# Out-projection of a hybrid trunk: seven products of 2x2 blocks with weight sums formed in memory, and a regrouped GLA output

## The chip, the cores and the metric

One core of a Trainium2 chip. The metric is the device time of one launch in microseconds. The core has TensorE (matrix products, PE in the profile; its weight loads are PEld), VectorE (DVE), ScalarE (ACT), GpSimd (POOL) and SyncE (SP, which here only starts transfers). Products gather in eight PSUM banks of 128 x 512 f32.

## What is computed

One layer of a trunk with three kinds of heads, on 512 tokens with 16 learned tokens ahead of them (528 in all), model width 2048, float32:

```python
h = rms_norm(x, norm_w)
proj = h @ w_in                            # 2048 x 7585
# columns of proj go to
#   6 gated DeltaNet heads   (q, k, v of 128; conv, silu; chunked delta rule)
#   5 GLA heads              (q, k of 64, v of 128; chunks of 64)
#   5 forgetting-attention heads ("fox"; q, k, v of 128; softmax with decay)
o_dn  = gated_head_norm(o_dn,  dz, dn_norm_w)     # normed o * w * silu(dz)
o_gla = gated_head_norm(o_gla, gz, gla_norm_w)
o_fox = o_fox * silu(fz)
o = concat([o_dn, o_gla, o_fox])[tokens]          # 512 x 2048, 16 heads of 128
y = x + o @ w_out                                 # 2048 x 2048
out = rms_norm(y, final_norm_w)                   # the 512 tokens
```

All large products are made in three: every operand is split into a float32r part (hi) and the rest (lo), and hi·hi, lo·hi and hi·lo are summed. One logical product of 128 x 128 by 128 x 512 is therefore three TensorE instructions.

## The kernel before, in words

**In-projection.** The 7585 columns go in 59 blocks of 128 columns (`inproj`, products on L168), in the order in which heads need them. Each block takes two weight tiles of 128 x 1024 (512 KB): `load_half` starts the transfer on SP's queue, and `split` makes the hi part by a ScalarE copy (L144) and the lo part by a VectorE subtraction (L145). raw, hi and lo have two buffers each. The result is transposed: rows are columns of the projection, columns are tokens.

**Heads.** DeltaNet heads go in two groups of three, then GLA heads in pairs (`gla_pair`), then the fox heads one by one (`fox_head`). Each head's gate block (`gate_z`) makes silu(z) into a 128 x 512 tile `zs`; GpSimd takes the first step of a silu (a maximum, L287), ScalarE three, VectorE the multiply. At a head's end its output is multiplied into that tile. In `gla_pair` the output `pgo` of each head is made of four 128-token blocks; for each block stands a product of 128 rows (L769, attention within the block) and behind it one of 64 rows (L770, the state).

**Order.** A scheduler places every engine's instructions by estimated times, splits ahead of other work. So in-projection products fill TensorE while heads wait on other engines, and under the last fox heads the out-projection's first quarter does.

**Out-projection.** w_out is taken in four quarters of 512 columns (`cc`), and in each over 16 heads and four blocks of 128 tokens: `mms` (L913) issues the three products. Two heads share a weight tile of 512 KB (`rawo`, `whio`, `wloo` are its raw, hi and lo), so a tile feeds 24 products. `split_o` splits each head's output once. The last two heads (`LAST = 14`) are held back: their products (`pz`) come at the end, token block by token block, so that the adds to the residual (L972), the squares (L974), the norm (L978 to L984) and the output transfers (L990) of one token block run under the products of the next. The residual x is loaded on ScalarE's queue into `acc`. In the last token block the last quarter is cut in two halves of 256.

Of the kernel before, what the change touches and what calls it, by code (L numbers as in the profile page):

```python
# [8 lines left out]
F32 = mybir.dt.float32  # L9
F32R = mybir.dt.float32r  # L10
# [8 lines left out]
P = 128  # L19
# [8 lines left out]
H = 3  # L28
# [4 lines left out]
DN_HEADS, GLA_HEADS, FOX_HEADS = 6, 5, 5  # L33
R0 = 32
# [43 lines left out]
def tile_hybrid_trunk(ctx, tc, xT, xtok, mtok, w_gate, w_in, w_out, consts, lmask, fin_w, out, dbg=None):  # L78
# [5 lines left out]
    hp = pool("hp", 2 * KT)  # L84
    wp = pool("wp", 2)
    zp = pool("zp", 11)
    six = pool("six", 8)
    wk = pool("wk", 2)
# [4 lines left out]
    def row(name, dt=F32):  # L93
        return wk.tile([P, 3 + T], dt, tag="row", bufs=7, name=name)
# [83 lines left out]

    done = {}
# [113 lines left out]
    zs = {}  # L293

    def gate_z(kind, h, t=None):
# [4 lines left out]
        if t is None:  # L300
            t = zp.tile([P, S], F32, tag="zs", name=f"zs{kind}{h}")
        silu(t, z[:, :S], f"{kind}{h}")
        zs[kind, h] = t
# [335 lines left out]
    def gla_pair(p):  # L639
# [125 lines left out]
        for e in range(ne):  # L765
            rr = slice(64 * e, 64 * e + 64)
            for b in range(NB):
                bs = slice(b * P, (b + 1) * P)
                PE.matmul(po[e][:, bs], at[:, e * NB + b, :], vt[:, e, bs], start=True, stop=False)  # L769
                PE.matmul(po[e][:, bs], qd[rr, bs], ss[b][rr, :], start=False, stop=True)  # L770
        for e in range(ne):
            f = wk.tile([P, NB], F32, tag="gso", name=f"gso{p}{e}")
            for b in range(NB):
                sq = wk.tile([P, P], BF16, tag="sq", name=f"gsq{p}{b}{e}")
                A.activation(sq, po[e][:, b * P : (b + 1) * P], AF.Square, accum_out=f[:, b : b + 1])
            A.activation(f, f, AF.Ln, scale=1.0 / P, bias=eps_c)
            A.activation(f, f, AF.Exp, scale=-0.5)
            on = qk[:, e, :S]
            for b in range(NB):
                A.activation(on[:, b * P : (b + 1) * P], po[e][:, b * P : (b + 1) * P], AF.Copy, scale=f[:, b : b + 1])  # L780
            pt = psm.tile([P, 512], F32, tag="m", name=f"pgt{p}{e}")
            for b in range(NB):
                PE.transpose(pt[:, b * P : (b + 1) * P], on[:, b * P : (b + 1) * P], ident)
            o = zs["gz", 2 * p + e]
            V.scalar_tensor_tensor(out=o, in0=pt, scalar=glw[:, 0:1], in1=o, op0=ALU.mult, op1=ALU.mult)


    def fox_head(h):
# [22 lines left out]
        cc = six.tile([P, 2 * T + S], F32, tag="six", name=f"fc{h}")  # L811
        z = wk.tile([P, S], F32, tag="gd", name=f"fz{h}") if h < 2 else cc[:, T + S : T + 2 * S]
        gate_z("fz", h, z)
# [53 lines left out]
        V.tensor_tensor(out=z, in0=po[:, :512], in1=z, op=ALU.mult)  # L867
# [10 lines left out]
    for h in range(GLA_HEADS):  # L878
        gate_z("gz", h)
# [8 lines left out]
    for p in range(3):  # L888
        gla_pair(p)
    for h in range(GLA_HEADS):  # L890
        dump(f"ogl{h}", zs["gz", h])
    for h in range(FOX_HEADS):
        fox_head(h)
    for h in range(FOX_HEADS):
        dump(f"ofx{h}", zs["fz", h])


    heads = [("dz", h) for h in range(DN_HEADS)] + [("gz", h) for h in range(GLA_HEADS)] \
        + [("fz", h) for h in range(FOX_HEADS)]
    oparts = []  # L900

    def split_o(i):
        z = zs[heads[i]]
        hi, lo = part(f"oh{i}"), part(f"ol{i}")
        A.copy(hi, z)
        V.tensor_tensor(out=lo, in0=z, in1=hi.bitcast(F32), op=ALU.subtract)
        oparts.append((hi, lo))

    def mms(p_, hi, lo, i, tb, first, last):
        s = slice(tb * P, (tb + 1) * P)  # L910
        oh, ol = oparts[i]
        for n, (o_, w_) in enumerate(((oh, hi), (oh, lo), (ol, hi))):
            PE.matmul(p_, o_[:, s], w_, start=(first and n == 0), stop=(last and n == 2))  # L913

    LAST = 14
    halves = lambda w: [[t[:, j * 512 : (j + 1) * 512] for t in w] for j in range(2)]
    acc, wl = {}, {}

    def load_last(c):
        raw = wp.tile([P, 1024], F32, tag="raw", name=f"rawl{c}")  # L920
        nc.sync.dma_start(out=raw, in_=w_out[c, LAST // 2])
        r = []
        for j in range(2):
            hi, lo = part(f"wlh{c}{j}"), part(f"wll{c}{j}")
            split(raw[:, j * 512 : (j + 1) * 512], hi, lo)
            r.append((hi, lo))
        return r

    for i in range(LAST):
        split_o(i)  # L930
    for cc in range(4):
        pa = [psb.tile([P, 512], F32, tag="b", name=f"pa{cc}{tb}") for tb in range(4)]
        for kp in range(LAST // 2):
            w = halves(load_half(w_out[cc, kp], f"o{cc}_{kp}"))
            for j in range(2):
                i = 2 * kp + j
                for tb in range(4):
                    mms(pa[tb], *w[j], i, tb, i == 0, cc < 3 and i == LAST - 1)
            if cc == 3 and kp % 2 and kp < 6:
                c = kp // 2  # L940
                wl[c] = load_last(c)
        for tb in range(4):
            if 4 * cc + tb < 11:
                a = zp.tile([P, S], F32, tag="zs", name=f"acc{cc}{tb}")
            else:
                a = six.tile([P, S], F32, tag="six", name=f"acc{cc}{tb}")
            nc.scalar.dma_start(out=a, in_=xtok[tb * P : (tb + 1) * P, cc * 512 : (cc + 1) * 512])
            if cc < 3:
                V.tensor_tensor(out=a, in0=a, in1=pa[tb], op=ALU.add)
            acc[tb, cc] = a  # L950
        if cc == 0:
            for i in range(LAST, KT):
                split_o(i)
    wl[3] = halves(load_half(w_out[3, LAST // 2], "l3"))
    fw = []
    for c in range(4):
        f = part(f"fw{c}").bitcast(F32)
        nc.scalar.dma_start(out=f, in_=fin_w[c * 512 : (c + 1) * 512].partition_broadcast(P))
        fw.append(f)
    ss = wk.tile([P, 4, 5], F32, tag="fss", bufs=1, name="fss")  # L960
    rr = wk.tile([P, 4], F32, tag="frs", bufs=1, name="frs")
    for tb in range(4):
        for cc in (3, 0, 1, 2):
            a = acc[tb, cc]
            cuts = 2 if (tb, cc) == (3, 2) else 1
            for n in range(cuts):
                c = slice(512 // cuts * n, 512 // cuts * (n + 1))
                p_ = pa[tb] if cc == 3 else psm.tile([P, 512], F32, tag="m", name=f"pz{tb}{cc}{n}")
                for j in range(2):
                    hi, lo = wl[cc][j]  # L970
                    mms(p_[:, c], hi[:, c], lo[:, c], LAST + j, tb, cc < 3 and j == 0, j == 1)
                V.tensor_tensor(out=a[:, c], in0=a[:, c], in1=p_[:, c], op=ALU.add)  # L972
                sq = row(f"sqf{tb}{cc}{n}")
                A.activation(sq[:, c], a[:, c], AF.Square, accum_out=ss[:, tb, cc + 2 * n : cc + 2 * n + 1])  # L974
            if cc != 2:
                G.tensor_tensor(out=a, in0=a, in1=fw[cc], op=ALU.mult)  # L976
        r = rr[:, tb : tb + 1]
        V.reduce_sum(r, ss[:, tb, : 3 + cuts], axis=mybir.AxisListType.X)  # L978
        A.activation(r, r, AF.Ln, scale=1.0 / D, bias=eps_c)
        A.activation(r, r, AF.Exp, scale=-0.5)  # L980
        for cc in (3, 0, 1, 2):
            a = acc[tb, cc]
            if cc == 0:
                A.activation(a, a, AF.Copy, scale=r)  # L984
            elif cc == 2:
                V.scalar_tensor_tensor(out=a, in0=a, scalar=r, in1=fw[cc], op0=ALU.mult, op1=ALU.mult)  # L986
            else:
                V.tensor_scalar_mul(a, a, r)  # L988
            q = nc.scalar if cc % 2 else nc.sync
            q.dma_start(out=out[tb * P : (tb + 1) * P, cc * 512 : (cc + 1) * 512], in_=a)  # L990
# [55 lines left out]
```

## Time and profile before

| | us |
|---|---|
| median of 3 runs | 1047.62 (1046.19 to 1048.34) |
| the profiled execution | 1048.64 |
| its span, first to last instruction | 1046.9 |
| TensorE busy | 1019.8, granted clock 0.991 |
| VectorE busy | 574.8 |
| ScalarE busy | 410.7 |
| GpSimd busy | 134.9 |

How to read it. The page's row of slices gives the busy share of each of 40 equal parts of the span in tenths, PEclk the clock that TensorE was granted. A group line gives: line, engine, operation, output<-inputs with shapes, count, then busy time in all and the mean of one in ns, then the engine's idle time just before them and what ended most of it. A line of the list of waits gives what waited for what, then us in total, times, and the longest. A line of the chain or the timeline starts with start and duration in us. A table of stretches gives each engine's busy time with its count of instructions, the granted clock, the DMA share and GB/s.

### The profile page before, as it was taken

The numbers are of one execution on the slowest core, as the hardware profiler recorded it, in microseconds if no ns is written. First come the engines' busy times: TensorE is split into PE (matmuls) and PEld (weight loads), VectorE is DVE, ScalarE is ACT, GpSimd is POOL, SyncE is SP. The second block draws the span as 40 slices with busy tenths as digits, with TensorE's granted clock in tenths as the row PEclk, the third lists the DMA queues.
The fourth block names the chain that finished last, engine by engine and source line by source line (L and its number), as shares of the span: only waits on it lengthen the run. The fifth ranks groups of instructions, "written<-read, shape, count | busy, mean of one in ns | idle before, by whom it ended". The sixth has DMA issues, their size and how long they took to land.

```text
span 1046.9 us, 19027 instructions
## 1 busy us (share of the span) xinstructions
PE 1019.8 (97%) x7787; PEld 914.5 (87%) x7787; DVE 574.8 (55%) x1251; ACT 410.7 (39%) x895; POOL 134.9 (13%) x137
## 2 busy tenths in 40 slices
PE   9999999999999999999999999999999999999994
PEld 7899999989999888899989878898989888888883
DVE  6366868855567972334828274455444474332437
ACT  6643533343455333244344443333323262222234
POOL 0021312220213131000100010110101010000014
PEclk9999999999999998999999999999999999999998
DMA  9613222223222322222212122222222263222424
GB/s 351 233 48 127 82 89 92 99 77 108 89 69 82 96 102 77 69 77 73 78 42 67 46 87 74 94 72 86 89 84 87 86 204 126 93 82 100 141 81 160
DMA packets 42347, 105.15 MB, mean 100 GB/s; under 512 B 10589, under 2 KB 13917, under 8 KB 42260
## 3 DMA queue, kind: packets, MB, share of 16 engines
q1 hardware_dynamic: 26848, 90.23, 24.6%
q10 hardware_dynamic: 15412, 13.70, 4.5%
q8 instruction: 61, 1.00, 0.4%
q14 instruction: 26, 0.21, 0.1%
HBM read 98.74 MB, written 5.05 MB: 99 GB/s over the span
## 4 chain that ended last, share of the span: by engine, by line
PE 54%; DVE 3%; ACT 1%; issue 1%; DMA 0%; DVEq 0%
PE pp L168 29%; PE pa L913 15%; PE pss L708 1%; PE pgo L770 1%; PE pfo L863 1%; PE pgo L769 1%; PE pfa L831 1%; PE pz L913 1%; DVE acc L988 1%; PE pfx L846 1%; ACT sqf L974 0%; PE pfd L832 0%; PE pfo L866 0%; DVE acc L986 0%; PE pgk L660 0%
## 5 line engine op out<-in xcount | busy, mean ns | idle before, releaser
L168 PE MATMUL pp<-xh,whi 128*128 128x264 f32 (+2 forms) x1456 | 378.5, 312 | 0.9 <-DVE vg L278 0.8
L168 PE MATMUL pp<-xh,wlo 128*128 128x264 f32 (+2 forms) x1456 | 376.8, 311 | 0.0
L168 PE MATMUL pp<-xl,whi 128*128 128x264 f32 (+2 forms) x1456 | 376.2, 310 | 0.0
L168 PEld LDWEIGHTS pp<-xh,whi 128*128 128x128 f32 x1456 | 244.5, 190 | 16.0 <-issue 1.4
L168 PEld LDWEIGHTS pp<-xl,whi 128*128 128x128 f32 x1456 | 245.2, 190 | 14.4 <-issue 1.4
L168 PEld LDWEIGHTS pp<-xh,wlo 128*128 128x128 f32 x1456 | 245.4, 190 | 13.3 <-issue 0.3
L145 DVE TENSOR_TENSOR wlo<-raw,whi 128x1024 fp32r<-128x1024 f32 x110 | 136.4, 1240 | 124.6 <-ACT whi L144 123.8
L144 ACT CAST whi<-raw 128x1024 fp32r<-128x1024 f32 x110 | 115.3, 1049 | 202.2 <-PE pp L168 181.1
L913 PE MATMUL pa<-whio,ol 128*128 128x512 f32 x224 | 88.0, 393 | 0.0
L913 PE MATMUL pa<-wloo,oh 128*128 128x512 f32 x224 | 87.9, 393 | 0.0
L913 PE MATMUL pa<-whio,oh 128*128 128x512 f32 x224 | 79.1, 396 | 0.0
L145 DVE TENSOR_TENSOR wloo<-rawo,whio 128x1024 fp32r<-128x1024 f32 x28 | 34.6, 1236 | 75.2 <-ACT whio L144 75.1
L144 ACT CAST whio<-rawo 128x1024 fp32r<-128x1024 f32 x28 | 29.4, 1049 | 93.7 <-PE pa L913 60.1
L913 PEld LDWEIGHTS pa<-whio,ol 128*128 128x128 f32 x224 | 42.1, 188 | 9.9
L913 PEld LDWEIGHTS pa<-wloo,oh 128*128 128x128 f32 x224 | 42.1, 188 | 9.5
L913 PEld LDWEIGHTS pa<-whio,oh 128*128 128x128 f32 x224 | 42.0, 188 | 9.2
L287 POOL TENSOR_SCALAR stc<-cv 128x528 f32<-128x528 f32 (+1 forms) x18 | 28.3, 1572 | 165.3 <-DVE cv L361 142.5
L361 DVE SCALAR_TENSOR_TENSOR cv<-pb,cpk,cv 128x528 f32<-128x528 f32 (+1 forms) x54 | 40.8, 755 | 0.6
L976 POOL TENSOR_TENSOR acc<-acc,fw 128x512 f32<-128x512 f32 x12 | 15.7, 1335 | 170.9 <-ACT sqf L974 170.9
L278 DVE TENSOR_TENSOR pb<-pp,rstd 128x264 f32<-128x264 f32 (+1 forms) x36 | 13.8, 424 | 26.2 <-PE pp L168 26.1
L456 DVE TENSOR_TENSOR ot<-ab 51x30 f32<-51x30 f32 (+14 forms) x60 | 20.3, 339 | 3.3 <-POOL stc L287 1.7
L458 DVE TENSOR_TENSOR ab<-ab,ot 51x30 f32<-51x30 f32 (+14 forms) x60 | 20.6, 343 | 1.5
(380 smaller groups left out, 1304.2 us busy)
## 6 DMA issues: line engine op xcount, KB each, us to landing
raw<-in_w_in SPq DMA_DIRECT2D x110, 512.0 KB, 3.2
rawo<-in_w_out SPq DMA_DIRECT2D x28, 512.0 KB, 3.2
xt<-in_xtok SPq DMA_DIRECT2D x8, 512.0 KB, 9.1
acc<-in_xtok ACTq DMA_DIRECT2D x16, 256.0 KB, 5.4
xs<-in_xT SPq DMA_DIRECT2D x7, 528.0 KB, 6.8
rawl<-in_w_out SPq DMA_DIRECT2D x4, 512.0 KB, 5.2
out<-acc SPq DMA_DIRECT2D x8, 256.0 KB, 2.5
out<-acc ACTq DMA_DIRECT2D x8, 256.0 KB, 2.6
```

The costliest lines, as they stand in the source:

```text
L144: A.copy(hi, raw)
L145: V.tensor_tensor(out=lo, in0=raw, in1=hi.bitcast(F32), op=ALU.subtract)
L168: PE.matmul(p_[:, :nt], wt[:, j * m : (j + 1) * m], xx[k][:, t0 : t0 + nt], start=(k == 0 and wt is hi and xx is xh), stop=(k == KT - 1 an ...
L278: V.tensor_tensor(out=o, in0=p_[rows], in1=rstd[rows, t0 : t0 + n], op=ALU.mult)
L287: G.tensor_scalar_max(t, src, LOW)
L361: V.scalar_tensor_tensor(out=c, in0=pb[:, t0 + w : w + T], scalar=cwc[:, blk, w : w + 1], in1=c, op0=ALU.mult, op1=ALU.add)
L456: V.tensor_tensor(out=t3, in0=a3[:, j + 1 :, j : j + 1].to_broadcast([NN * 4 + H, m, j]), in1=a3[:, j : j + 1, 0:j].to_broadcast([NN * 4 + ...
L458: V.tensor_tensor(out=a3[:, j + 1 :, 0:j], in0=a3[:, j + 1 :, 0:j], in1=t3, op=ALU.add)
L708: PE.matmul(ps[o0 : o0 + n, b * n : b * n + n], kx[rr, k0 : k0 + n], qx[rr, q0 : q0 + n], start=True, stop=True)
L769: PE.matmul(po[e][:, bs], at[:, e * NB + b, :], vt[:, e, bs], start=True, stop=False)
L913: PE.matmul(p_, o_[:, s], w_, start=(first and n == 0), stop=(last and n == 2))
L976: G.tensor_tensor(out=a, in0=a, in1=fw[cc], op=ALU.mult)
```

## The change

**Out-projection.** Tokens are cut in two halves of 256, heads in two halves of eight, and two column quarters (`ca`, `cb`) make a pair. For each of the two pairs the 2x2 product of blocks is made by seven products of blocks instead of eight (a form of Strassen's scheme): a and f use plain blocks on both sides (a with its sign changed), b, c and e sums on both sides, d a sum of weights, g a sum of operands. Each product sums eight heads for two token blocks of 128 (`product`, `mms`). In PSUM, y gathers a and c, later e and g; z gathers b and d; intermediate values are added to or subtracted from several `acc` tiles (`add`).

**Weight sums.** Four sums of weight quarters for each pair, 2 MB each, are formed in device memory: a copy from w_out or from an earlier sum on SP's queue, then an accumulating transfer on GpSimd's queue, each in two parts of 1 MB and in pieces of 512 bytes. One of these steps is issued with each in-projection block from the 15th on; sum4's are eight blocks later than the rest. `load_w` loads tiles of 512 KB of a quarter or a sum; 56 are loaded, and each feeds 12 products. raw and hi have three buffers, lo two.

**Operands.** The sums of head outputs are made on VectorE (`sub`) and split by `put` (a ScalarE copy and a VectorE subtraction of 256 columns): n11, n1, t2, x22, n3, x21, n4, each of eight heads. The first nine heads' outputs are written to device memory (`spill`) and loaded again, two or three times, on GpSimd's queue (`load_o`), as is the residual.

**Gate blocks.** The gates of GLA heads 3 and 4 and of all fox heads are projected after the last fox head's other blocks; these heads' outputs are copied (`og`, `of`) and multiplied by silu(z) later.

**GLA grouping.** The products of `pgo` come in another order: those of 128 rows of both heads first, then those of 64 rows, the two heads (rows 0 to 63 and 64 to 127) in turn.

**The end.** The pair's product g is made token block by token block from kept weights (`last_w`), the last token block in halves of 256.

The order in which the program's instructions stand on each engine: by in-projection blocks counted from 0, one accumulation stands at block 26, four in a row at block 32 ahead of the `eg` multiplies (the decay times queries) of the second DeltaNet group, three at block 37 ahead of GLA's second `gkd`, four at block 44 around fox head 0's small copies, and the four of sum4 at blocks 50, 54, 54 and 58 between the last gates' maxima and the reloads. On ScalarE the copies of x22 stand ahead of the first weight tile's copy.

```diff
+    wsum = {(pr, n): drp.tile([4, P, 1024], F32, name=f"sum{n}_{pr}") for pr in range(2) for n in (1, 2, 3, 4)}
+    quarter = lambda pr, n: w_out[2 * pr + n // 2, 4 * (n % 2) : 4 * (n % 2) + 4]
...
+                def copy(pr=pr, h_=h_):
+                    tc.keep_in_program_order(nc.sync.dma_start(
+                        out=rows_of(wsum[pr, n][h_]), in_=rows_of(first(pr)[h_]), max_dma_last_dim=512))
...
+                def plus(pr=pr, h_=h_):
+                    tc.keep_in_program_order(nc.gpsimd.dma_start(
+                        out=rows_of(wsum[pr, n][h_]), in_=rows_of(then(pr)[h_]), accum_op=ALU.add,
+                        max_dma_last_dim=512))
...
+    one, three = list(sum_steps(1, q_(2), q_(3))), list(sum_steps(3, q_(0), q_(2)))
+    two, four = list(sum_steps(2, lambda pr: wsum[pr, 1], q_(0))), list(sum_steps(4, lambda pr: wsum[pr, 2], q_(1)))
+    steps = one[:4] + three[:4] + one[4:] + three[4:] + two + 8 * [lambda: None] + four
...
         if key not in done:
+            begun_blocks.append(key)
+            if len(begun_blocks) > 14 and steps:
+                steps.pop(0)()
...
         for e in range(ne):
-            rr = slice(64 * e, 64 * e + 64)
             for b in range(NB):
                 bs = slice(b * P, (b + 1) * P)
-                PE.matmul(po[e][:, bs], at[:, e * NB + b, :], vt[:, e, bs], start=True, stop=False)
-                PE.matmul(po[e][:, bs], qd[rr, bs], ss[b][rr, :], start=False, stop=True)
+                PE.matmul(po[e][:, bs], at[:, e * NB + b, :], vt[:, e, bs], start=b == 0, stop=False,
+                          skip_group_check=True)
+        for b in range(NB):
+            bs = slice(b * P, (b + 1) * P)
+            for e in range(ne):
+                rr = slice(64 * e, 64 * e + 64)
+                PE.matmul(po[e][:, bs], qd[rr, bs], ss[b][rr, :], start=False, stop=b == NB - 1,
+                          skip_group_check=True)
...
-        V.tensor_tensor(out=z, in0=po[:, :512], in1=z, op=ALU.mult)
+        o = zs["fz", h] = zp.tile([P, S], F32, tag="zs", name=f"of{h}")
+        A.copy(o, po[:, :512])
...
+    def put(op, i, src, sign=1.0):
+        hi, lo = (t[:, i] for t in op)
+        if sign > 0:
+            A.copy(hi, src)
+            V.tensor_tensor(out=lo, in0=src, in1=hi.bitcast(F32), op=ALU.subtract)
...
+    for h in range(GLA_NOW, GLA_HEADS):
+        gate_z("gz", h, zs["gz", h])
+    for h in range(FOX_HEADS):
+        gate_z("fz", h, zs["fz", h])
+    for i in range(KP):
+        a, b = load_o(i, "oa")
+        put(n11, i, a, -1.0)
+        put(n1, i, sub(f"d1_{i}", a, b))
+    for i in range(KP):
+        a, b = load_o(i, "ob")
+        c, d = load_o(KP + i, "oc")
+        u = sub(f"d2_{i}", a, b)
+        V.tensor_tensor(out=u, in0=u, in1=d, op=ALU.add)
+        put(t2, i, u)
...
+        put(x22, i, d)
+        put(n3, i, sub(f"d3_{i}", b, d))
+        put(x21, i, c)
...
+        product("a", y, n11, quarter(pr, 0), True, False)
...
+        product("b", z, n1, wsum[pr, 1], True, False)
...
+        product("c", y, t2, wsum[pr, 2], False, False)
...
+        product("d", z, x22, wsum[pr, 4], False, True)
...
+        product("e", y, n3, wsum[pr, 3], False, False)
...
+        product("f", w_, x21, quarter(pr, 1), True, True)
...
+        if pr == 0:
+            product("g", y, n4, quarter(pr, 3), False, True)
...
+                    for i in range(KP):
+                        mms(y[tb], n4, last_w[i], i, tb, False, n == cuts - 1 and i == KP - 1, cs)
```

More of the change, by code (lines that the diff above doesn't have):

```diff
@@ L877, in tile_hybrid_trunk @@
         dn_mix(g, st)
-    for h in range(GLA_HEADS):
+        for h in range(H * g, H * g + H):
+            spill(h)
+    for h in range(GLA_NOW):
         gate_z("gz", h)
@@ L889, in tile_hybrid_trunk @@
         gla_pair(p)
+        for h in range(2 * p, min(2 * p + 2, GLA_NOW)):
+            spill(DN_HEADS + h)
     for h in range(GLA_HEADS):
@@ L915, in tile_hybrid_trunk @@
[L915 to L976, printed above, removed]
@@ new lines, in tile_hybrid_trunk @@
+    late.close()
+    tp2 = pool("tp2", 8, reuse_waits="tile")
+    wq = pool("wq", 3, reuse_waits="tile")
+    x22, n3, x21, n4 = (operand(tp2, n) for n in ("x22", "n3", "x21", "n4"))
+    for i in range(KP):
+        a, b = load_o(i, "od")
+        c, d = load_o(KP + i, "oe")
+        put(x22, i, d)
+        put(n3, i, sub(f"d3_{i}", b, d))
+        put(x21, i, c)
+        u = sub(f"d4_{i}", c, d)
+        v = sub(f"d5_{i}", a, b)
+        V.tensor_tensor(out=u, in0=u, in1=v, op=ALU.subtract)
+        put(n4, i, u)
@@ new lines, in load_w, with mms @@
+    def load_w(src, i, name):
+        raw = wq.tile([P, 1024], F32, tag="raw", name=f"raw{name}{i}")
+        nc.sync.dma_start(out=raw, in_=src[i])
+        hi = wq.tile([P, 1024], F32R, tag="hi", name=f"whi{name}{i}")
+        lo = wq.tile([P, 1024], F32R, tag="lo", bufs=2, name=f"wlo{name}{i}")
+        split(raw, hi, lo)
+        return [(hi[:, c], lo[:, c]) for c in (slice(0, 512), slice(512, 1024))]
+    def mms(p_, op, w, i, tb, first, last, cs=slice(0, 512)):
+        s = slice(tb * P, (tb + 1) * P)
+        (oh, ol), (wh, wl) = op, w
+        for n, (o_, w_) in enumerate(((oh, wh), (ol, wh), (oh, wl))):
+            PE.matmul(p_[:, cs], o_[:, i, s], w_[:, cs], start=first and n == 0, stop=last and n == 2,
+                      skip_group_check=True)
@@ new lines, in tile_hybrid_trunk, with new_acc @@
+    ss = rw.tile([P, 4, 5], F32, tag="fss", name="fss")
+    rr = rw.tile([P, 4], F32, tag="frs", name="frs")
+    acc, fw, more = {}, [], []
+    def new_acc(tb, c):
+        if len(acc) < 11:
+            a = zp.tile([P, S], F32, tag="zs", name=f"acc{tb}{c}")
+        else:
+            if len(acc) in (11, 15):
+                more[:] = [tp1.tile([P, KP * HS], F32R, tag="t", name=f"accs{len(acc)}").bitcast(F32)]
+            n = (len(acc) - 11) % 4
+            a = more[0][:, n * S : (n + 1) * S]
+        nc.gpsimd.dma_start(out=a, in_=xtok[tb * P : (tb + 1) * P, c * 512 : (c + 1) * 512])
+        acc[tb, c] = a
@@ new lines, in add, with square, times_fw, final @@
+    def add(tb, c, p_, op=ALU.add, cs=slice(0, 512)):
+        a = acc[tb, c]
+        V.tensor_tensor(out=a[:, cs], in0=a[:, cs], in1=p_[:, cs], op=op)
+    def square(tb, c, n=None, cs=slice(0, 512)):
+        n = c if n is None else n
+        sq = row(f"sqf{tb}{c}{n}")[:, cs]
+        A.activation(sq, acc[tb, c][:, cs], AF.Square, accum_out=ss[:, tb, n : n + 1])
+    def times_fw(tb, c):
+        a = acc[tb, c]
+        G.tensor_tensor(out=a, in0=a, in1=fw[c], op=ALU.mult)
+    def final(tb, last, n=4):
```

164 lines of the change are left out of this document (128 added, 36 removed).

## The prediction

> **What bounds the kernel now.** I read the page first: busy times, slices, shares of the chain, groups.
>
> ```profile
> span 1046.9 us, 19027 instructions
> PE 1019.8 (97%) x7787; PEld 914.5 (87%) x7787; DVE 574.8 (55%) x1251; ACT 410.7 (39%) x895; POOL 134.9 (13%) x137
> PE   9999999999999999999999999999999999999994
> PEclk9999999999999998999999999999999999999998
> DMA  9613222223222322222212122222222263222424
> PE 54%; DVE 3%; ACT 1%; issue 1%; DMA 0%; DVEq 0%
> L145 DVE TENSOR_TENSOR wlo<-raw,whi 128x1024 fp32r<-128x1024 f32 x110 | 136.4, 1240 | 124.6 <-ACT whi L144 123.8
> L144 ACT CAST whi<-raw 128x1024 fp32r<-128x1024 f32 x110 | 115.3, 1049 | 202.2 <-PE pp L168 181.1
> ```
>
> TensorE is busy in every slice but the last, at the full clock, and DMA has no share in the chain. Only the number of products, their spacing, and holes count. The list of waits says the same of the weights: the copy of a tile waits for the products to free a buffer.
>
> ```profile
> ACT whi L144 <- PE pp L168: 181.1, 75, 5.6
> ACT whio L144 <- PE pa L913: 60.1, 17, 4.5
> ACT whio L144 <- DMA rawo<-in_w_out: 7.8, 1, 7.8
> ```
>
> Then three places. In the chain, the longest piece of the out-projection gives a product's price; the table of stretches shows no hole there; the timeline shows GLA's output products and the end.
>
> ```profile
> 899.46 83.66 PE pa L913 x362
> ```
>
> ```profile
> 850.00:1000.00 150.00, 150.00 (x662) 122.15 (x661) 58.15 (x93) 39.14 (x56) 3.55 (x3) 1.00 0.35 119
> 1020.00:1047.00 27.00, 13.37 (x63) 10.60 (x61) 19.04 (x26) 11.80 (x36) 12.97 (x10) 0.85 0.43 155
> ```
>
> ```profile
> 532.18 0.88 PE L759 MATMUL pgn<-gvt,kdt 128*64 128x128 f32 x12
> ...
> 537.79 0.49 PE L769 MATMUL pgo<-gvt,kq 128*128 128x128 f32 x2
> 538.21 0.48 PE L770 MATMUL pgo<-gs,gqd 64*128 64x128 f32 x2
> 538.62 0.49 PE L769 MATMUL pgo<-gvt,kq 128*128 128x128 f32 x2
> ...
> 1033.51 0.28 PE L913 MATMUL pz<-wlh,ol 128*128 128x256 f32 x1
> ...
> 1037.71 1.33 DVE L972 TENSOR_TENSOR acc<-acc,pz 128x512 f32<-128x512 f32 x3
> ...
> 1039.97 0.16 DVE L978 TENSOR_REDUCE frs<-fss 128x1 f32<-128x5 f32 x1 [0.93 <-ACT sqf L974]
> ```
>
> 83.66 us for 362 products of 512 columns is 0.231 us each. Products of 128 and of 64 rows take turns every 0.42 us. After the last product's start 13.4 us pass to the span's end, the first 4.2 because VectorE comes late to the last add.
>
> The profiled execution took 1048.64 us: 1046.9 of span and 1.7 outside. It is 1.0 above the median, 1047.62. I sum against 1048.64 and take 1.0 off. The three runs spread over 2.2 us, so about 0.2% is what a measurement can tell.
>
> **Products: -22.** Before: 4 column quarters x 4 token blocks x 16 head blocks x 3 = 768 products of 512. After: 2 pairs x 7 products x 8 head blocks x 2 token blocks x 3 = 672 (some in halves). 96 x 0.231 = 22.2 us off a fully busy engine.
>
> **GLA's grouping: -8.** 16 output products took 6.7 us (534.44 to 541.12), 0.42 each; the 40 cost 16.7. After, products of 128 rows stand together, then the 64-row ones, the two row halves in turn. For 128 rows in a row the bound is DeltaNet's L577, 0.67 us for three, 0.223 each: 20 x 0.223 = 4.5. For 64 rows in turn, from 0.135 (the 12 records, six products, of L759 in 0.81 us) to 0.223: 2.7 to 4.5. So 7.2 to 8.9 instead of 16.7; I take -8. If the 64-row loads don't overlap, 0 to -4.
>
> **The end: -3.5.** The last token block now has one half's add and square after its last product, with VectorE up to date: from that add to the end took 9.2 us before, of 13.1 after the start of the last product. Between 0 and -4; -3.5.
>
> **Gate blocks: 0 for the products.** Seven blocks of 48 products move behind the fox heads' other blocks; they fill TensorE under the last fox heads, as the out-projection's first quarter did. Their silus become a separate copy and a multiply: seven VectorE operations of 512 (0.65 us) beside 78 us of products, covered by the 45% in which VectorE is idle.
>
> **The seam: +6.** The out-projection used to begin with operands ready. Now the copies of x22 wait for the last gate block's last product, and on ScalarE they stand ahead of the copy of the first weights, together with one silu step and operand copies of reloaded heads: some 11 operations of about 0.40 us (the square of 256 columns at 1039.05 is 0.40) and the weights' 1.05. VectorE's part (six operations of 0.33 and 1.24) runs alongside. That is 5 to 6 us without a product; below it 3 (some copies done earlier), above it whatever the reloads add. I take 6. In the last stretch of the table, half idle, the granted clock is 0.85; a hole of 6 us may cost 2 or 3 us more in slow products, which I leave to the range. The Trainium skill ("TensorE: Matmul & The Clock Gate", "What's actually happening") states that one idle window of about 3.4 us drops the clock to half until a busy window; by it the hole would add an estimated 1.7 us, and the row of 0.85 agrees in direction.
>
> **VectorE in the first five products: +6.** A weight tile now feeds 12 products (2.77 us), not 24. In the first column pair VectorE must also build t2, x22, n3, x21 and n4. From the first tile's subtraction to the sixth product's first stand 20 subtractions of 1.24, 10 adds of 0.67 and about 85 of 256 columns at 0.33 to 0.36 (the 1.33 us for one 512 and two 256 at 1037.71): 60 to 62 us, against 20 x 2.77 = 55.4 us of products. Stall 5 to 7 if the order is kept without slack; 0 if it starts with a lead. In the second pair it has 1.24 of 2.77 and no operands: no stall.
>
> **Loads: 0.** 56 tiles of 512 KB at 2.77 us are 189 GB/s; the highest slice moved 351. A tile lands in 3.2 us with three buffers ahead.
>
> **Sums in memory: +3.** 16 copies of 1 MB go on SP's queue, 16 accumulating transfers on POOL's, in pieces of 512 bytes. Nothing like either is in the trace. For the transfer, 2048 pieces over 16 engines: by q10 (15412 packets, 4.5% of 16 spans, 49 ns each) 6.3 us, by q1 (153 ns) 19.6. A copy ahead of a weight tile on SP delays it by that; a tile is asked for some 11 us before it is needed and lands in 3.2, so 6.3 is covered and 19.6 shows. For POOL's own time the ends are 0.34 us (an ACT-queue issue at 1030.84) and 19.6; below nothing is excluded, work is only added. Behind POOL's transfers stand the eg multiplies of the second DeltaNet mix (four ahead of them), GLA's gkd (three), fox 0's copies, gate maxima and reloads of heads. POOL idles long there: before, from 423.2 to 435.8 ahead of the first eg, whose products start at 443.7, so about 19.5 us of cover; from 532.8 to 562.7 ahead of the second gkd. Up to about 5 us each all is covered; I take that and allow +3 for collisions. The Trainium skill ("DMA: Bandwidth & Descriptors", "Anatomy of one DMA") fits a transfer from GpSimd's queue at 2.0 us plus its bytes by 436 GB/s, an estimated 4.4 us for 1 MB. By it the term would also be 3 or less; no trace of before has such a transfer.
>
> **Sum.** 1048.6 - 22.2 - 8 - 3.5 + 6 + 6 + 3 = 1029.9; minus 1.0, about 1029. Own range 1021 to 1038.
>
> **Rivals.**
> - All hidden: no seam, VectorE in the lead, sums free: 1029 - 15 = 1014 (1011 to 1019). For it: VectorE idles 45%. Against it: the copies of x22 can't start before the last gate block ends. 0.13.
> - Transfers collide with loads: each of the 32 MB-sized transfers costs 0.5 us of late weights instead of 0.1, 1029 + 13 = 1042 (1036 to 1052). For it: the copies are ahead of weights in SP's own queue, and the low share of DMA now is no measure for 512-byte pieces. Against it: 11 us of tolerance. 0.13: 0.07 still faster, 0.03 the same, 0.03 slower.
> - **Slower: POOL held by each accumulation.** If POOL prepares 2048 pieces by its own program for 10 us (midway between 0.34 and 19.6), four ahead of the first eg take 40 us of 19.5 covered: +20. The three ahead of gkd take 30 of 30: 0. At the seam the reloads of heads stand behind two, and one is ahead of a gate maximum: 3 x 10 less a block's 11 us, +19. 1029 + 39 - 3 = 1065 (1050 to 1085). It decides from about 7.5 us each (30 - 19.5 + 22.5 - 11 = 22). For it: nothing in the trace bounds that price. Against it: POOL is busy 13%. The Trainium skill ("SBUF — State Buffer", "SBUF: two separate sides") adds that VectorE's two-port modes keep GpSimd from writing descriptors; a row of before, two L988 scalings at 1.51 us beside a busy POOL and 0.88 later, shows the two engines do meet. 0.29.
> - GLA's grouping does nothing: 1037. Against it: L577 and L759 show shorter spacing where kinds don't alternate. 0.03.
>
> **How the numbers follow.** The forecast has 0.42. Faster: 0.42 + 0.13 + 0.07 + 0.03 = 0.65; same 0.03; slower 0.29 + 0.03 = 0.32. The range runs from 1013 (the upper two thirds of the best case) to 1066 (half of POOL's case); about 0.2 lies outside.
>
> **What would show it.** After: 1782 + 63 products of 512 and 256 columns instead of 1896 + 27 over the whole kernel; the chain's pieces at 0.23 a product; GLA's pgo group in runs of 0.22 or less; a hole of some 6 us between the last gate block and the first product of a, released by ScalarE's first weight copy; late weights waiting for VectorE in the first pair and none in the second; the last add 9 us before the end. I am wrong if the waits list names eg, gkd, stfz or the reloads with tens of us (POOL held), raw tiles behind DMA (collision), or if the first pair shows no VectorE wait.

## The result, and the profile after

The changed kernel takes 1079.53 us (median of 4 runs, 1073.33 to 1080.61), against 1047.98 before: a ratio of 1.0278, 95% interval 1.0219 to 1.0336. I forecast 1029 us and a gain; it is a loss of some 30 us, 13 us above the top of the range. The profiled execution took 1073.33 us, the least of the four; the stretches below are read from it, and where the other 6 us of the median stand no trace shows.

The page after: span, busy times, slices, queues, shares of the chain, issues with their median time to landing.

```profile
span 1071.6 us, 19283 instructions
PE 1007.2 (94%) x7709; PEld 901.0 (84%) x7709; DVE 627.9 (59%) x1368; ACT 446.8 (42%) x963; POOL 190.5 (18%) x195
PE   9999999999999999699999989999999966989996
...
PEclk9999999999999999899999999999999987999998
DMA  9613222356435636935771495225332698766765
...
q0 software_dynamic: 36384, 27.79, 15.8%
...
PE 59%; DMA 8%; DVE 7%; issue 3%; ACT 2%; POOL 1%; ACTq 0%; DVEq 0%; POOLq 0%; SPq 0%
...
sum<-in_w_out POOLq DMA_DIRECT2D x16, 1024.0 KB, 17.7
sum<-in_w_out SPq DMA_DIRECT2D x8, 1024.0 KB, 6.6
```

TensorE's row now has holes: at the 17th slice (430 to 455 us) and at the 33rd and 34th (860 to 910), where the granted clock falls too. DMA has 8% of the chain instead of none. A 1 MB copy from w_out lands in 6.6 us (8.4 from an earlier sum); a 1 MB accumulation takes 17.7, by the median.

Where the time went. Between two marks that both traces have, I take how much longer the stretch became, and how much in-projection work (0.231 us for each product of 512 columns) it lost or gained; the difference is stall. From the last state product of the second DeltaNet group's inverse (`ps`) to that group's last output product (`po`), the stretch that I call the mix, before took 59.4 us and after 60.5, but after runs 13.3 us fewer of in-projection products there: 14.4 us of stall. From trace to trace, stretches in which the kernels don't differ vary by up to 5 us ahead of the mix and by up to 1.5 from the mix on. The same count over the span, and the out-projection against 672 x 0.231 = 155.3:

| | us |
|---|---|
| span, before to after | +24.7 |
| products left out | -22.2 |
| GLA's output products | -7.9 |
| end, from the last product's start (13.4 to 10.1) | -3.3 |
| second DeltaNet mix | +14.4 |
| fox head 0 | +6.5 |
| seam (in-projection to out-projection), from the last fox output to the first product of a | +22.5 |
| out-projection, 167.4 for 155.3 | +12.1 |
| the rest, +24.7 less all of these | +2.6 |

**The seam.** First the chain of waits there (start, length), then TensorE's, ScalarE's and GpSimd's timelines.

```profile
849.99 19.77 DMA sum<-sum
...
871.47 17.84 DMA oa<-od
```

```profile
894.25 0.79 PE L1031 MATMUL py<-whia,n11h 128*128 128x512 f32 x1 [13.47 <-ACT whia L148]
```

```profile
889.33 0.42 ACT L969 ACTIVATE n11h<-oa 128x256 fp32r<-128x256 f32 x1 [11.34 <-DMA oa<-od]
```

```profile
870.39 1.89 POOL L201 DMA_DIRECT2D sum<-in_w_out  x1 [2.29 <-DMA sum<-sum]
871.47 1.95 POOL L977 DMA_DIRECT2D oa<-od  x2
```

The last copy of a sum needs 19.8 us while accumulations fill the DMA engines (the engines' busy share is 1.25 and 1.26 in the two stretches of 10 us from 860 on); in the run below that leaves those accumulations out, the same copy takes 6.3. The accumulation that adds to it goes out at 870.4, and behind it in GpSimd's queue two reloads of head outputs, which take 17.8 us. ScalarE waits for those to make n11, and the first weights' copy stands behind that on ScalarE. TensorE has no product for 13.5 us.

**The mix.** TensorE in two stretches of it after, then the same work before (busy us and instructions of PE, PEld, DVE, ACT, POOL; clock; DMA share; GB/s).

```profile
440.00:450.00 10.00, 4.21 (x25) 3.68 (x26) 2.28 (x8) 3.38 (x13) 0.99 (x1) 0.85 0.97 129
450.00:460.00 10.00, 7.18 (x37) 6.49 (x37) 3.48 (x13) 3.42 (x16) 0.00 (x0) 0.67 0.10 22
```

```profile
450.00:460.00 10.00, 10.00 (x86) 9.92 (x85) 4.68 (x14) 4.70 (x18) 1.01 (x1) 1.00 0.01 2
```

Before, 228 in-projection products stand in the program's order between the first `psn` and the last `po` of that group; after, 132. The other 96 are the two GLA gate blocks. Without them the group's own chain of small steps lies open. One step has also become slower: a transfer of `eg` issued among the accumulations took 6.5 us instead of 3.4. ScalarE's timeline:

```profile
446.49 0.52 ACT L614 ACTIVATE eg<-eg 128x384 f32<-128x384 f32 x1 [4.57 <-DMA eg<-gd]
```

**GLA and the end.** TensorE's timeline where the alternating products stood, and the last instructions:

```profile
526.25 1.95 PE L812 MATMUL pgo<-gvt,kq 128*128 128x128 f32 x16
528.13 0.49 PE L818 MATMUL pgo<-gs,gqd 64*128 64x128 f32 x4
528.45 0.84 PE L818 MATMUL pgo<-gsn,gqd 64*128 64x128 f32 x12
529.22 0.40 PE L172 MATMUL pp<-xh,wlo 128*128 128x264 f32 x1
...
1061.51 0.28 PE L1031 MATMUL py<-wl,n4h 128*128 128x256 f32 x1
...
1061.82 0.42 DVE L1051 TENSOR_TENSOR accs<-accs,py 128x256 f32<-128x256 f32 x1 [0.61 <-PE py L1031]
```

Sixteen products take 2.97 us instead of 6.7: 0.235 us for one of 128 rows, 0.136 for one of 64. The last add starts 0.3 us after the last product instead of 4.2.

### The profile page after: what moved, and what is told of

It reads as the page before. It is cut to its first block, busy times and chain, and to the rows that moved or that the text cites. A ratio compares the mean times of both kernels' runs of the same rounds, so it can differ in the third digit from the quotient of the medians.

```text
span 1071.6 us, 19283 instructions
## 1 busy us (share of the span) xinstructions
PE 1007.2 (94%) x7709; PEld 901.0 (84%) x7709; DVE 627.9 (59%) x1368; ACT 446.8 (42%) x963; POOL 190.5 (18%) x195
## 3 DMA queue, kind: packets, MB, share of 16 engines
q0 software_dynamic: 36384, 27.79, 15.8%
## 4 chain that ended last, share of the span: by engine, by line
PE 59%; DMA 8%; DVE 7%; issue 3%; ACT 2%; POOL 1%; ACTq 0%; DVEq 0%; POOLq 0%; SPq 0%
PE pp L172 40%; PE py L1031 6%; PE pw L1031 2%; DMA sum<-sum 2%; DMA oa<-od 2%; DMA sc<-ab 1%; PE pz L1031 1%; DMA eg<-gd 1%; PE pss L752 1%; DMA rawc<-sum 1%; DVE d L982 1%; PE pfa L882 1%; PE py L628 1%; PE pfo L914 1%; ACT whi L148 1%
## 5 line engine op out<-in xcount | busy, mean ns | idle before, releaser
L172 PEld LDWEIGHTS pp<-xl,whi 128*128 128x128 f32 x1456 | 245.7, 190 | 14.5 <-issue 0.8
L201 POOL DMA_DIRECT2D sum<-in_w_out x16 | 30.8, 2317 | 10.3 <-issue 8.0
L1031 PE MATMUL py<-whia,n11h 128*128 128x512 f32 x32 | 13.5, 421 | 13.5 <-ACT whia L148 13.5
L886 DVE CUSTOM_DVE_ANT_0 fp<-pfa,fc 128x16 f32<-128x16 f32 (+3 forms) x20 | 7.4, 368 | 31.6 <-PE pfa L882 31.6
L900 ACT CAST fphi<-pfx 128x384 fp32r<-128x384 f32 (+2 forms) x20 | 8.0, 400 | 36.4 <-PE pfx L897 36.4
L323 POOL TENSOR_SCALAR stdz<-zdz 128x512 f32<-128x512 f32 x6 | 11.2, 1874 | 65.8 <-DVE zdz L341 65.8
L874 POOL CAST ptmhi<-zero_c 128x512 fp32r<-128x512 f32 x5 | 3.9, 773 | 102.8 <-PE pfo L914 102.8
L891 ACT ACTIVATE fp<-fp,fsm 128x144 f32<-128x144 f32 (+3 forms) x20 | 11.5, 576 | 24.8 <-DVE fsm L890 24.4
L773 POOL TENSOR_TENSOR gkd<-gkd,gqk 128x512 f32<-128x512 f32 (+1 forms) x3 | 9.9, 3304 | 62.1 <-ACT gkd L772 62.1
## 6 DMA issues: line engine op xcount, KB each, us to landing
sum<-in_w_out POOLq DMA_DIRECT2D x16, 1024.0 KB, 17.7
```

Source lines behind the costliest of these rows:

```text
L172: PE.matmul(p_[:, :nt], wt[:, j * m : (j + 1) * m], xx[k][:, t0 : t0 + nt], start=(k == 0 and wt is hi and xx is xh), stop=(k == KT - 1 an ...
L201: tc.keep_in_program_order(nc.gpsimd.dma_start(out=rows_of(wsum[pr, n][h_]), in_=rows_of(then(pr)[h_]), accum_op=ALU.add, max_dma_last_dim ...
L323: G.tensor_scalar_max(t, src, LOW)
L891: A.activation(pr[:, : m + P], pr[:, : m + P], AF.Exp, bias=sm[:, 2:3], accum_out=sm[:, 3:4])
L1031: PE.matmul(p_[:, cs], o_[:, i, s], w_[:, cs], start=first and n == 0, stop=last and n == 2, skip_group_check=True)
```

## The experiments

Three theories. One: the transfers of the sums cost the time. Two: the moved gate blocks were the cover of the mix (and of fox head 0). Three: ScalarE's and VectorE's work on operands bounds seam and out-projection. Ratios are to the kernel before, on the same chip.

**GLA's grouping alone, on the kernel before.** The edit is the hunk of the diff that reorders `pgo`.

> The kernel before with the regrouped GLA output products alone. The trace of the changed kernel lost 15.05 - 7.1 = 7.9 us of work there against before, so about 1048 - 8 = 1040 us. Rival: the 8 us came from something that was moved at the same time (fewer products of the in-projection among them), then 1044 to 1048.

1041.78 us, ratio 0.9922 (0.9904 to 0.9941): 8 us, all of it the grouping's. Of the versions that leave nothing out it is the fastest, faster than both kernels.

**No sums.**

```diff
-    steps = one[:4] + three[:4] + one[4:] + three[4:] + two + 8 * [lambda: None] + four
+    steps = []
...
-        product("b", z, n1, wsum[pr, 1], True, False)
+        product("b", z, n1, quarter(pr, 2), True, False)
```

(and the same for c, d and e)

> The changed kernel without any copy or accumulating transfer; b, c, d and e multiply plain weight quarters, so the product is not the reference's. Theory 1 (the transfers cost the time: they fill the DMA engines, and the reloads queue behind them on GpSimd's queue): the hole of 13.5 us before the out-projection and those of 4.6 and 1.5 before it fall to some 6 in all, the hole of 3.8 us at fox head 0 goes with its slow clock, and the loads of eg are fast again: 1073 - 18 - 6 - 4 = 1045 us. Theory 2 (the moved gate blocks took their products out of the second DeltaNet mix, where they covered its chain): the mix still has holes of 6 us or more and a low clock, whatever the transfers do. Theory 3 (ScalarE's and VectorE's own work at the seam is the bound): the seam keeps 15 us or more, 1065 us.

1043.14 us, ratio 0.9946 (0.9919 to 0.9972). The transfers cost 36 us. The hole at the seam is 3.7 us, with the same work on ScalarE and VectorE:

```profile
866.92 0.50 PE L1031 MATMUL py<-whia,n11h 128*128 128x512 f32 x1 [3.74 <-ACT whia L148]
```

So theory three falls for the seam. But fox head 0's hole stays, 6.8 us by the same count, and the mix keeps 7.0 of its 14.4: these are not the transfers'.

**GLA's gate blocks back.**

```diff
-GLA_NOW = 3
+GLA_NOW = 5
```

> The changed kernel with GLA's gate blocks 3 and 4 back ahead of the GLA heads (five of the seven gate blocks last). Theory 2: the second DeltaNet mix has its 96 products between again, its holes (10 us) and its slow clock (4 us) go: 1073 - 14 = 1059 us, seam unchanged. Theory 1 alone: the four accumulations at the mix still make its loads late, the holes stay at 5 us or more: 1070 us.

1066.73 us, ratio 1.0161 (1.0130 to 1.0193), 13 us less. The 228 products stand in the mix again, and its stall is gone (-0.4 us by the same count), with the DMA share as high as 0.63:

```profile
450.00:460.00 10.00, 9.56 (x82) 9.38 (x82) 2.61 (x9) 3.22 (x11) 1.02 (x1) 1.00 0.63 201
460.00:470.00 10.00, 10.00 (x87) 10.00 (x86) 6.07 (x16) 4.77 (x18) 1.01 (x1) 1.00 0.45 141
```

Late transfers do no harm there under cover; theory two holds for the mix. That the gain comes close to the mix's 14.4 us is chance: the seam's stall also fell, from 22.5 to 11.2 us, 4.3 of which came back just ahead of it, and the out-projection grew from 167 to 175.

**Copies without accumulations; without the last four accumulations.**

```diff
-                yield plus
+                yield lambda: None
```

```diff
-    steps = one[:4] + three[:4] + one[4:] + three[4:] + two + 8 * [lambda: None] + four
+    steps = one[:4] + three[:4] + one[4:] + three[4:] + two + 8 * [lambda: None] + four[:4]
```

> The changed kernel with the 16 copies but without the 16 accumulating transfers (the sums hold one term only). Theory 1, with the accumulations as the cause: within 3 us of the kernel without either, about 1046 us, since a copy alone lands in 6.6 us. If the copies in SyncE's queue are what delays the weights, it stays at 1060 us or more.

> The changed kernel without the four accumulations of the last sum, the ones at the seam (one term of that sum is left out); the other twelve and all copies stay. If these four make the seam's hole, it falls from 13.5 us to 6 or less, and with it the holes before it: about 1061 us. If the sixteen accumulations cost alike wherever they stand (together about 32 us), a quarter goes: 1071 us.

1046.90 us, ratio 0.9983 (0.9958 to 1.0008), and 1060.27, ratio 1.0101 (1.0068 to 1.0133). The 16 copies cost some 4 us, the 16 accumulations 33. Four of them, those at the seam, cost 19: it is their place, not a price for each. Without them the seam's hole is again small:

```profile
880.88 0.50 PE L1031 MATMUL py<-whia,n11h 128*128 128x512 f32 x1 [3.75 <-ACT whia L148]
```

The other twelve cost 13 us, most of it at the mix (15.8 us of stall with them, 5.4 without).

**The last sum eight blocks earlier**, on the kernel with GLA's gate blocks back.

```diff
-    steps = one[:4] + three[:4] + one[4:] + three[4:] + two + 8 * [lambda: None] + four
+    steps = one[:4] + three[:4] + one[4:] + three[4:] + two + four
```

> The gate blocks of GLA heads 3 and 4 back in their place (as in the run before of that name, 1066.7 us) and the pause of eight blocks ahead of the last sum's steps left out, so that no accumulation stands beside the seam. If the seam's hole is the reloads behind the last accumulations, some 18 us go: about 1050 us, the hole before the first product of the out-projection at 6 us or less. If every accumulation costs its 2 us wherever it stands, it stays at 1064 us.

1067.13 us, ratio 1.0189 (1.0140 to 1.0238): no gain. The stall from the last fox output to the first product fell from 11.2 to 6.3 us, but a net of 3 were lost again before it, and the out-projection remained at 175 us. Three of the four accumulations now go out in a row (729 to 732 us) under fox head 1, and the stretches of fox heads 1 and 2 have 5.6 us more of stall. With GLA's blocks gone from the end, that out-projection is longer (167 in the changed kernel; its first pair takes 93 us instead of 86): which fits operands that had been built under gate blocks and are now built under its own products; that was not tested.

**Pieces of 4 KB.**

```diff
-    rows_of = lambda t: t.rearrange("k p (a c) -> (k p a) c", a=2)
+    rows_of = lambda t: t.rearrange("k p c -> (k p) c")
...
-                        out=rows_of(wsum[pr, n][h_]), in_=rows_of(first(pr)[h_]), max_dma_last_dim=512))
+                        out=rows_of(wsum[pr, n][h_]), in_=rows_of(first(pr)[h_]), max_dma_last_dim=4096))
...
-                        max_dma_last_dim=512))
+                        max_dma_last_dim=4096))
```

> The changed kernel with copies and accumulations in pieces of 4 KB instead of 512 bytes, all else the same. If the number of pieces sets their price (in the changed kernel 33000 packets on GpSimd's queue took 65 ns each, 8.3 us of all 16 engines for 1 MB), an eighth of the pieces at no more than 200 ns is 3 us: the accumulations land in some 8 us instead of 17.7, and the time comes to about 1055 us. If the bytes set it, no change: 1078 us. If weights wait behind larger pieces, 1085 us or more.

1066.02 us, ratio 1.0163 (1.0130 to 1.0195), 13 us less, half of what was expected from the number of pieces. GpSimd's queue took 11.2% of the engines' time instead of 15.8 (3.4 of each is reloads and residual), the accumulations landed in 13.2 us. An eighth of the pieces took 0.63 of the accumulations' engine time. If that time is a part for each piece and a part for the bytes, the bytes were some 58% of it.

```profile
q0 software_dynamic: 7712, 27.79, 11.2%
...
sum<-in_w_out POOLq DMA_DIRECT2D x16, 1024.0 KB, 13.2
```

**The first reloads on ScalarE's queue.**

```diff
-            nc.gpsimd.dma_start(out=t, in_=od[i])
+            (nc.scalar if name == "oa" else nc.gpsimd).dma_start(out=t, in_=od[i])
```

> The changed kernel with the eight reloads of the first operand on ScalarE's queue instead of GpSimd's. If the reloads are late because they stand behind accumulations in one queue, the hole of 13.5 us falls to 6 or less: about 1071 us. If they are late because the accumulations fill the engines that all queues share (share over 1 in that stretch), they still take 10 us or more and the time stays at 1077 us or more.

1075.18 us, ratio 1.0259 (1.0227 to 1.0292). The reloads landed in 7.4 us instead of 15.3, and the hole stayed at 14.5, though the whole seam's stall fell from 22.5 to 14.9 us. The list of waits at the seam tells what took their place:

```profile
POOL sum L201 <- DMA sum<-sum: 15.7, 1, 15.7
ACT stfz L324 <- POOL stfz L323: 15.1, 3, 12.8
```

GpSimd now stands 15.7 us at the last accumulation until its copy has landed; behind it on that engine is a gate's maximum, behind that ScalarE's silu step, and behind it the first weights' copy. Neither outcome that I had named: the queue was one of two ways by which the same accumulation holds the seam.

**Operand sums on GpSimd.**

```diff
-        V.tensor_tensor(out=d, in0=a, in1=b, op=ALU.subtract)
+        G.tensor_tensor(out=d, in0=a, in1=b, op=ALU.subtract)
```

> The changed kernel with the 48 subtractions that form operand sums on GpSimd instead of VectorE, some 16 us less of VectorE's 62 in the first five products. If VectorE bounds the first pair, its 85.9 us fall by 4 or more: about 1074 us. If late weight tiles bound it, no change within 2 us: 1079 us; and GpSimd, slower at this, could make it worse.

1081.07 us, ratio 1.0321 (1.0288 to 1.0355), and the first pair took 90.0 us instead of 85.9. It settles nothing on VectorE: one subtraction took 0.72 to 2.31 us on GpSimd, against 0.34 from start to start on VectorE.

**No lo parts for five operands, without sums.**

```diff
-        return [pl.tile([P, KP, HS], F32R, tag="t", name=f"{name}{n}") for n in ("h", "l")]
+        hi, lo = [pl.tile([P, KP, HS], F32R, tag="t", name=f"{name}{n}") for n in ("h", "l")]
+        return [hi, lo] if name in ("n11", "n1") else [hi, hi]
...
-            V.tensor_tensor(out=lo, in0=src, in1=hi.bitcast(F32), op=ALU.subtract)
+            if op[0] is not op[1]:
+                V.tensor_tensor(out=lo, in0=src, in1=hi.bitcast(F32), op=ALU.subtract)
```

> The kernel without sums (run before, 1043 us), with the lo parts of five of the seven operands left out (their hi part stands in for them, as many products): about 40 VectorE subtractions of 0.34 us less in the first five products. If VectorE is what makes the seven products of the first pair take 82.5 instead of 77.6 us there, they come to 79 or less: 1039 us. If late tiles are, no change: 1043 us.

1040.17 us, ratio 0.9920 (0.9896 to 0.9944). The intervals of this and of the kernel without sums meet, so the time alone decides nothing. The first pair does: from a of the first pair to a of the second, 82.5 us without sums, and here 78.2, against 77.6 of products; the two runs without accumulations at the seam, with all lo parts, took 81.4 and 82.2. TensorE's timelines, without sums and then without the lo parts too:

```profile
866.92 0.50 PE L1031 MATMUL py<-whia,n11h 128*128 128x512 f32 x1 [3.74 <-ACT whia L148]
949.46 0.39 PE L1031 MATMUL py<-whia,n11h 128*128 128x512 f32 x1
```

```profile
875.65 0.80 PE L1033 MATMUL py<-whia,n11h 128*128 128x512 f32 x1 [5.08 <-ACT whia L148]
953.86 0.39 PE L1033 MATMUL py<-whia,n11h 128*128 128x512 f32 x1
```

VectorE's work costs the first pair some 4 us, as its count of instructions said.

**Gates back, without sums.** `GLA_NOW = 5`, fox head 0's gate inside `fox_head`, no sums.

> The kernel without sums (1043 us) with the gate blocks of GLA heads 3 and 4 and of fox head 0 back in their place. If cover is all that is missing at the DeltaNet mix and at fox head 0 there, both holes close: 7 + 6 us, about 1031 us. If the blocks only move a hole to the end of the in-projection, 1043 us. It bounds what seven products can bring here.

1050.16 us, ratio 1.0010 (0.9987 to 1.0032): 7 us more than with the seven blocks last, where I expected 12 less. Both holes did close (0.2 and 0.5 us of stall). But the out-projection took 174 us instead of 168, and TensorE idled where the seven blocks had stood:

```profile
840.00:850.00 10.00, 6.55 (x32) 4.85 (x30) 4.09 (x16) 2.31 (x6) 0.81 (x1) 0.94 0.25 96
850.00:860.00 10.00, 6.63 (x19) 4.74 (x19) 7.37 (x15) 7.57 (x18) 5.14 (x6) 0.55 0.02 3
860.00:870.00 10.00, 5.35 (x13) 3.85 (x14) 8.43 (x18) 8.51 (x19) 7.58 (x13) 0.66 0.87 284
```

The gate blocks are one cover for two places.

**Sums spread out**: begun ten blocks earlier, a free block after each accumulation; with the three gate blocks back and 4 KB; with the gates last and 4 KB; with the gates last and 512 bytes.

```diff
+    gap = lambda adds: [s for a_ in adds for s in (a_, lambda: None)]
-    steps = one[:4] + three[:4] + one[4:] + three[4:] + two + 8 * [lambda: None] + four
+    steps = one[:4] + three[:4] + gap(one[4:]) + gap(three[4:]) + two[:4] + gap(two[4:]) + four[:4] + gap(four[4:])
...
-            if len(begun_blocks) > 14 and steps:
+            if len(begun_blocks) > 4 and steps:
```

> Three things together: the gate blocks of GLA heads 3 and 4 and of fox head 0 back in their place, pieces of 4 KB, and the sums begun ten blocks earlier with a free block after every accumulation, the last of them well ahead of the seam. If bursts of accumulations and their place are the cost, most of it goes: some 14 us at the DeltaNet mix, 6 at fox head 0, 15 at the seam, of 1079: about 1044 us. If each accumulation costs about 1.5 us wherever it stands, 16 x 1.5 stay on top of the kernel without sums and with its gates back: 1055 us or more.

> The changed kernel, its seven gate blocks last, with the sums begun ten blocks earlier, a free block after every accumulation, and pieces of 4 KB. If the price of the accumulations is their bursts and their place at the seam, most of the 36 us between the changed kernel (1079) and the one without sums (1043) goes: about 1053 us. If it is their bytes and their instructions, wherever they stand, 1065 us or more.

> The same as the run before it with pieces of 512 bytes. If the place alone decides, within 2 us of it: about 1054 us. If pieces decide too (in the changed kernel 4 KB alone brought 13 us), 1060 us or more.

1061.55 us, ratio 1.0147 (1.0090 to 1.0204); 1077.32, ratio 1.0274 (1.0237 to 1.0312); 1073.91, ratio 1.0229 (1.0199 to 1.0259). In the first, the sums cost 11 us over the same gates without sums, instead of 36; which of the three things did it is not separated. In the other two nothing clear of the spread was gained on the changed kernel. In the middle run the last accumulation goes out 12 us ahead of the reloads and the seam's stall is 4.7 us (22.5 in the changed kernel), but the mix stalls 24.6 us. Two things meet there. The order has only 84 in-projection products left in the mix (132 in the changed kernel). And two accumulations go out at 426 and 427, just ahead of it, and land after 12.4 and 20.0 us; a transfer of `eg` that starts at 434 lands among them only at 447.5, GpSimd's multiply waits for it, and TensorE stands 8.5 us for the multiply. After that it runs at half the clock for 20 us. The middle run, TensorE's timeline and three stretches:

```profile
449.50 0.80 PE L644 MATMUL po<-s,eg 128*128 128x128 f32 x2 [8.47 <-POOL eg L618]
```

```profile
440.00:450.00 10.00, 1.53 (x10) 1.34 (x11) 1.03 (x4) 0.52 (x1) 1.00 (x1) 0.65 0.52 151
450.00:460.00 10.00, 7.16 (x32) 6.32 (x31) 2.60 (x10) 3.43 (x17) 0.99 (x1) 0.50 0.12 20
460.00:470.00 10.00, 7.09 (x32) 6.50 (x32) 1.47 (x6) 3.58 (x17) 0.00 (x0) 0.50 0.08 21
```

Moving transfers moved products in the scheduler's order, and it brought other accumulations to the mix. The last two runs' intervals overlap, so what 4 KB pieces bring to spread sums stays open.

## Why the prediction was wrong

**Gate blocks, "0 for the products": the step that failed first.** I counted where the blocks went to and not what they had covered where they stood. They had filled the second DeltaNet mix: 14.4 us of stall, of which 7.0 without any sum transfer; with two blocks back in place none of it is left, with the sums (-0.4) or without (0.2). The order of the instructions showed it beforehand, 132 products instead of 228. Fox head 0's 6.5 us has the same source: before, 37 in-projection products stand between its first score products and the first transpose, after none; with its gate back (and no sums) the stall is 0.5.

**Sums in memory, "+3": the term that was most wrong, 36.** Of the 50 us between forecast and result 33 are this term's. For GpSimd's own time I took up to 5 us; it measured 1.9 (30.8 for all 16), and my rival of a POOL held 10 us by each is wrong in that. For the transfer I named 6.3 to 19.6 us and took it as covered: a copy lands in 6.6, an accumulation in 17.7, the first of a burst in 10 and the last in 21 to 25. What I did not ask is what waits for the transfer: at the seam the reloads in its queue, which the list of waits names with 21.7 us at ScalarE's n11; at the mix the transfer of `eg`. The fit of the Trainium skill ("DMA: Bandwidth & Descriptors", "Anatomy of one DMA"), an estimated 4.4 us for 1 MB from GpSimd's queue, is not what an accumulation in memory took here: 10 us as the first of a burst, 17.7 in the median. That VectorE keeps GpSimd from writing descriptors, as the Trainium skill has it ("SBUF — State Buffer", "SBUF: two separate sides"), does not show in an issue of 1.9 us.

**The slower rival was right in its outcome and in one of its places.** It put +20 on the mix, 0 on gkd and +19 on the seam by reloads that stand behind accumulations. The seam lost 19 us to those four, but by the transfers: by the queue and, once the reloads are moved, by GpSimd's wait for the copy. That the two 19 agree is luck. At the mix, the `eg` multiplies were not held; the transfer of `eg` was late, and cover was missing.

**The seam, "+6".** Without accumulations beside it, 3.7 us. The step was right, and my bound below it, 3, was closer. After the hole of 13.5 us the clock is 0.62 from 890 to 900, so the drop that I left to the range is there. The rule of the Trainium skill that I quoted ("TensorE: Matmul & The Clock Gate", "What's actually happening": an idle window halves the clock) agrees with the rows of 0.50 behind the hole of 8.5 us in the last experiment.

**VectorE in the first five products, "+6".** 8.3 us in the changed kernel (85.9 for 77.6; the slow clock after the seam's hole is in it), 4.9 without sums, and 4.3 of these go with the lo parts. Right. "No stall" in the second pair was wrong: 81.5 us for 77.6, with tiles of c late by their transfer (7.2 us to landing instead of 4.5 for others). TensorE lost 0.8 us behind them (2.5 without sums), so "Loads: 0" is short by that; where the rest of those 4 stands is open.

**Products, GLA, end.** -22.2 by count; -7.9 for -8, confirmed alone; -3.3 for -3.5.

**What the change can bring.** With the sums left out, it runs at 1043 us, and GLA's grouping alone at 1042. The 22 us of products and 3 of the end are spent on the mix (7.0), fox head 0 (6.8), the seam (4.2) and the out-projection's own stalls (12.7) before the sums cost anything.

## What to carry to other kernels

When work is moved, ask first what it was covering where it stood: on an engine that is busy 97% of the time, a block of independent products is also the cover of every chain beside it, and it covers one place only. A saving in products is then an upper bound, to be set against each new wait at its own place. A transfer in the background is free only as long as nothing that the next product needs stands behind it, in its queue, on its engine, or on the DMA engines it fills.

## What the runs showed of the hardware that I had not expected

- An accumulating transfer of 1 MB between places in memory took 17.7 us by the median (512-byte pieces, bursts of three or four: 10 us for the first of a burst, 21 to 25 for the last), 12.8 spread out, 8.9 to 9.6 spread out in 4 KB pieces; a plain copy of the same bytes 6.6 to 8.4. By the queues' shares, with and without sums, an accumulation's packet of 512 bytes took 64 ns of an engine (12.4% of 16 spans, 33000 packets), so 8.2 us of all 16 engines for 1 MB.
- TensorE takes 0.42 us for each f32 product of 128 columns when products of 128 and 64 rows alternate, and 0.235 and 0.136 when each kind stands together, the 64-row ones switching between the two row halves. It is not that a product adds to the columns which the one ahead of it has just written: DeltaNet's output products before (L598, L599) do that too, with 128 rows each, and start every 0.22 us.
- After a hole of 8.5 us TensorE stayed at a granted clock of 0.50 for 20 us, although its row was busy for 71% of that time.
